# An RWKV and neighbourhood-attention layer: small matmul jobs moved between stages, GpSimd products moved to VectorE, filler matmuls redistributed

## The chip, the cores and the metric

The kernel runs on one core of one Trainium2 chip. The metric is the device time of one execution in microseconds (us). The engines, with the short names of the profile, are TensorE (PE; its weight loads are PEld), VectorE (DVE), ScalarE (ACT), GpSimd (POOL) and SyncE (SP), which here issues nearly all the DMAs.

## The reference

One layer for 128 context tokens and 512 latent tokens, 640 in all, with D = 1024. A normed and modulated input is projected; one part of the projection feeds neighbourhood attention, another an RWKV-7 recurrence of eight heads, run forwards and backwards; both are gated, merged, projected out, and a gated feed-forward network follows.

```python
def _wkv_step(s, inp):
    r, w, k, v, a, b = inp
    sa = jnp.einsum("bhvk,bhk->bhv", s, a)
    s = s * w[:, :, None, :] + sa[..., None] * b[:, :, None, :] + v[..., None] * k[:, :, None, :]
    return s, jnp.einsum("bhvk,bhk->bhv", s, r)
```

The context part starts from a zero state and returns its final states, the latent part starts from given states. In both directions k and the decay differ. All arithmetic is fp32; large products are made of three matmuls on operands split into a high and a low part.

## The kernel before, in words

The 640 tokens are ten chunks of 64. The recurrence is done chunk by chunk: within a chunk it needs the inverse of a unit triangular 64 x 64 matrix, and between chunks a state is carried. A group `ct` of four is two heads (128 partitions). The ten chunks in two directions are 20 "lines". All of this lies in the block `s3`, and for each `ct` has these stages:

- `main`: loads the start states, and the **n jobs** (`n_job`, L990 on) compute the matrices to be inverted, on TensorE, for the lines in three lumps of 8, 8 and 4 (`parts8`). ScalarE copies each result to `Nt` (L1001). They need `AG`, which `akr` (L979) makes on VectorE.
- `inv`: VectorE transposes `Nt` to `RL` (L1082) and eliminates in 30 steps (L1096, L1110 with L1114, L1103); each step is a few VectorE instructions, each of which needs the one before. Then `RT` and `T` (L1123, L1125). At three steps given by `jobs` a lump of further matmuls is placed on TensorE: **v jobs** (transposes of v, copied by ScalarE to `ZV` at L1042; those of backward lines, `flip`, read what the forward lines wrote), **t jobs** (transposes of `BK`, copied to `TG` at L1065), and a **Gram lump** (`g_job`, L1010 and L1013). VectorE multiplies the lump by masks (L1020, L1023) `md` steps after it. After the steps come two small matmul rounds (L1135, L1150) that complete the inverse; I call this stretch the tail.
- `carry`: eight steps over the chunks. In each, TensorE multiplies by `AG` (L1181), ScalarE copies (x0, L1184), TensorE multiplies by the inverse (L1206), ScalarE copies to `ZV` (L1212), TensorE sums the next state (L1219) and the output (L1236), and VectorE scales the state by the decay (L1231), which the next step's L1181 reads.
- Beside the carry runs `prep` for the next group (`prep_a`, `prep_b`): decays by a scan, normed keys, `NK`, `BK`, `bv`. Its pieces are emitted between carry steps, as many as the budgets `bud` allow for ScalarE and VectorE. At the eighth step `last()` emits what is left of it, then `akr` and `r_` of the next group. Two products of each `prep_b` were GpSimd's: the second half of `BK` (L655) and, in the second direction, `bv` (L663).
- `out`: group norm, bonus and gate of the group, emitted beside the next group's `main` and `inv`, as is `bonus` (L962 to L970).

**Fillers.** Independent large matmuls (L173, tiles `fl`) are put between all of this: gates (g), the k, r and v projections of the next group, and the merge with the attention output (a, b). They are units of 48 (g, k, r, v), 24 (a) and 18 (b) matmuls in the fixed order `PRM["order"]`. `stream` hands them out one at a time; `weave` goes through the stage's generator and takes from `plan`, for every `yield`, a group `fillers.out.bonus` (in the carry `fillers.budget`). A unit can have to wait for a mark (v of the next group waited for the end of `inv`), and `need` pulls a unit through where its result is wanted. What follows a unit's matmuls on ScalarE and VectorE (a copy, a shift at L492 to L495, the merge at L1319 and L1322) is emitted some ticks later (`later`, `tick`). The next unit's weights are split on ScalarE (L154) and GpSimd (L155, a "cast") when an eighth of the current unit is done.

The order on every engine is the order in which the instructions are written (`tc.manual_schedule` for this block), so an instruction that waits holds all behind it on its engine. The attention output is loaded back by `o_load` when the last gate is done, just ahead of unit a0. Behind the block come the last merge (`last_gen`) and the projections, where TensorE is near full.

## Time and profile before

| | |
|---|---|
| time, median of 3 runs | 1306.46 us (1304.97 to 1311.55) |
| the profiled execution | 1306.15 us, its span 1304.4 us |
| PE busy | 1224.4 us, 94% |
| DVE busy | 677.3 us, 52% |
| ACT busy | 468.5 us, 36% |
| POOL busy | 282.5 us, 22% |
| mean granted clock of PE | 0.976 |
| block s3 in the span | about 281 to 760 us |

Times of rows are us from the start of the span. In a timeline row stand start, duration, engine, line, operation, output and inputs, shapes and count, and in brackets the idle time of the engine before it and what ended that. In a row of groups stand count, busy us, mean ns of one, and after the second bar the idle time before them.

### The profile page before, as it was taken

What the parts mean: (1) busy time and instruction counts of PE and PEld (TensorE: products, weight loads), DVE (VectorE), ACT (ScalarE), POOL (GpSimd) and SP (SyncE); (2) the same over time, 40 slices, a digit from 0 to 9 for tenths busy, and PEclk for the clock granted to TensorE, in tenths of its full rate; (3) what the DMA queues carried; (4) which work ended last, traced back from release to release, by engine and by line L of the source; (5) the groups of instructions that cost most, each with busy time, mean ns of one, the idle gap of its engine ahead of it and who ended that gap; (6) DMA issues with size and microseconds to landing.
All of it is one profiled execution on the core that took longest, in us unless ns stands there. A gap on an engine that the chain in (4) does not pass through costs nothing.

```text
span 1304.4 us, 27117 instructions
## 1 busy us (share of the span) xinstructions
PE 1224.4 (94%) x11418; PEld 1072.4 (82%) x11418; DVE 677.3 (52%) x1464; ACT 468.5 (36%) x969; POOL 282.5 (22%) x296
## 2 busy tenths in 40 slices
PE   6999999998898797989879989999999999999998
PEld 4688667688887696888768868899999889999987
DVE  4654566647647945874675294643333234333332
ACT  4544455644353345435422341632232111222210
POOL 1231455353223223322321570300000000000000
PEclk8999999999898999989989999999999999999999
DMA  9423975331111121121152472222122222122221
GB/s 347 148 71 123 295 235 166 126 117 45 54 47 49 59 65 44 34 88 45 38 208 89 131 277 82 97 81 82 66 74 88 66 80 81 65 66 95 68 90 41
DMA packets 54130, 134.36 MB, mean 103 GB/s; under 512 B 6868, under 2 KB 21716, under 8 KB 51960
## 3 DMA queue, kind: packets, MB, share of 16 engines
q1 hardware_dynamic: 53144, 131.43, 30.2%
q8 instruction: 90, 1.47, 0.5%
q10 hardware_dynamic: 864, 1.20, 0.3%
q14 instruction: 32, 0.26, 0.1%
HBM read 118.28 MB, written 14.32 MB: 102 GB/s over the span
## 4 chain that ended last, share of the span: by engine, by line
PE 51%; DVE 6%; issue 1%; ACT 1%; DMA 1%; POOL 1%; SPq 0%; DVEq 0%; ACTq 0%; POOLq 0%
PE f L173 24%; PE acc L260 15%; PE fl L173 5%; DVE pr L1110 1%; DVE RL L1114 1%; DVE vp L493 1%; PE w L1181 1%; DMA o<-o_d 1%; PE w L1219 0%; PE w L1193 0%; PE w L1206 0%; PE w L1135 0%; PE w L998 0%; PE w L1013 0%; DVE AG L979 0%
## 5 line engine op out<-in xcount | busy, mean ns | idle before, releaser
L173 PE MATMUL f<-h,whi 128*128 128x256 f32 (+1 forms) x1408 | 306.3, 309 | 0.6 <-POOL h L163 0.6
L173 PEld LDWEIGHTS f<-h,whi 128*128 128x128 f32 x1408 | 236.6, 189 | 1.1 <-POOL h L163 1.0
L154 ACT CAST whi<-wst 128x1024 fp32r<-128x1024 f32 (+2 forms) x134 | 132.3, 990 | 241.9 <-PE acc L260 108.6
L173 PE MATMUL f<-h,wlo 128*128 128x384 f32 (+1 forms) x704 | 217.6, 309 | 0.0
L155 DVE TENSOR_TENSOR wlo<-wst,whi 128x1024 fp32r<-128x1024 f32 x95 | 118.7, 1252 | 178.5 <-ACT whi L154 178.2
L173 PE MATMUL fl<-h,whi 128*128 128x320 f32 x736 | 180.4, 327 | 4.4 <-ACT U L487 3.3
L173 PEld LDWEIGHTS fl<-h,whi 128*128 128x128 f32 x736 | 129.1, 196 | 9.6 <-ACT U L487 3.5
L173 PEld LDWEIGHTS f<-h,wlo 128*128 128x128 f32 x704 | 133.0, 189 | 0.0
L173 PE MATMUL fl<-h,wlo 128*128 128x320 f32 x368 | 120.6, 328 | 1.4 <-POOL wlo L155 1.4
L155 POOL TENSOR_TENSOR wlo<-wst,whi 128x1024 fp32r<-128x1024 f32 (+2 forms) x39 | 79.6, 2041 | 161.8 <-ACT whi L154 158.7
L260 PE MATMUL acc<-whi,ul 128*128 128x512 f32 (+1 forms) x230 | 88.6, 385 | 0.0
L260 PE MATMUL acc<-whi,uh 128*128 128x512 f32 (+1 forms) x230 | 88.3, 386 | 0.0
L260 PE MATMUL acc<-wlo,uh 128*128 128x512 f32 (+1 forms) x230 | 88.2, 386 | 0.0
L260 PE MATMUL acc<-whi,h 128*128 128x512 f32 x240 | 80.6, 409 | 0.7 <-DVE h L369 0.7
L173 PEld LDWEIGHTS fl<-h,wlo 128*128 128x128 f32 x368 | 72.1, 196 | 4.3 <-POOL wlo L155 1.7
L173 PE MATMUL fl<-o,whi 128*128 128x320 f32 x224 | 57.3, 335 | 8.3 <-DMA o<-o_d 5.4
L173 PE MATMUL mm<-h,whi 128*128 128x320 f32 x256 | 63.9, 327 | 0.4 <-ACT pre L576 0.4
L1231 DVE TENSOR_TENSOR ZV<-w,Dt 64x128 f32<-64x128 f32 x64 | 18.4, 288 | 79.8 <-PE w L1219 78.6
L1611 DVE SCALAR_TENSOR_TENSOR a<-a,f 128x384 f32<-128x384 f32 (+1 forms) x44 | 21.5, 488 | 69.6 <-PE f L173 69.5
L260 PEld LDWEIGHTS acc<-whi,h 128*128 128x128 f32 x240 | 45.4, 191 | 14.0 <-issue 2.4
L260 PE MATMUL acc<-whi,m 128*128 128x512 f32 x160 | 53.0, 407 | 0.6 <-POOL m L1498 0.4
L162 ACT CAST uh<-a 128x384 fp32r<-128x384 f32 (+1 forms) x44 | 20.1, 458 | 87.6 <-DVE a L1611 87.6
(315 smaller groups left out, 2290.2 us busy)
## 6 DMA issues: line engine op xcount, KB each, us to landing
wst<-in_w_dram SPq DMA_DIRECT2D x66, 512.0 KB
wa<-in_w_ada_dram SPq DMA_DIRECT2D x16, 1024.0 KB
wst<-in_w_rw_dram SPq DMA_DIRECT2D x31, 512.0 KB
wst<-in_w_qkv_dram SPq DMA_DIRECT2D x12, 512.0 KB
o<-o_d SPq DMA_DIRECT2D x14, 320.0 KB
x<-in_xs_dram SPq DMA_DIRECT2D x8, 512.0 KB
wa<-in_w_ada_dram SPq DMA_DIRECT2D x16, 256.0 KB
wa<-in_w_ada_dram SPq DMA_DIRECT2D x8, 512.0 KB
```

Of the source, the lines that this page charges most:

```text
L154: act.copy(hi[:, :n], st[:, :n])
L155: (eng or dve).tensor_tensor(out=lo[:, :n], in0=st[:, :n], in1=hi[:, :n].bitcast(F32), op=ALU.subtract)
L162: act.copy(hi, src)
L173: pe.matmul(ps[:, :t1 - t0], w[:, a:a + 128], x[:, k0 + kt, t0:t1], start=n == 0, stop=n == 3 * nk - 1)
L260: pe.matmul(pss[i][:, a:b], x[:, kt, ts_], w[:, cs_], start=ki == 0 and n == 0, stop=ki == last and n == 2)
L493: dve.scalar_tensor_tensor(out=o, in0=U[:, u - 1:u - 1 + n], scalar=col("mu0", ci), in1=o, op0=ALU.mult, op1=ALU.add)
L1110: dve.tensor_tensor(out=prv, in0=V(RL[:, s + 1 + a, :], [[32, b - a], [0, s]], s), in1=V(RL[:, s, :], [[0, b - a], [1, s]]), op=ALU.mult)
L1114: dve.tensor_tensor(out=dst, in0=dst, in1=prv, op=ALU.add)
L1181: pe.matmul(px[hrows[h], g * 64:g * 64 + 64], AG[:, l, h, :], ZV[:, l, h, :], start=True, stop=True)
L1231: dve.tensor_tensor(out=V(ZV[own, l + 1, h, :], [[128 * dl, 2], [1, 64]]), in0=V(pn[own, :], [[64, 2], [1, 64]], 64 * g), in1=V(Dt[own, 0, ...
L1611: dve.scalar_tensor_tensor(out=a, in0=a, scalar=0.5, in1=p3[:, :n], op0=ALU.mult, op1=ALU.mult)
```

## The change

- v and t jobs leave the steps of `inv` and stand in `main`, ahead of the n jobs. The v jobs go by the ranges `partsv`, so that the flip of lines 10 and 11 is one of them and no longer part of a t job. v of the next group now waits for the bonus alone (`vR`).
- The Gram lumps are placed after steps 1, 5 and 9 instead of 2, 9 and 16, and their masks three steps later instead of two.
- For ct 1 to 3 the products of L655 and L663 are VectorE's, each with a cost of 0.8 in the budget; so is the addition of the merge at L1322.
- The plan: for ct 0 to 2 `main` has 12 fillers instead of 28, `inv` 231 or 233 instead of 165, `carry` 76 instead of 128 (the six after each step are gone). For ct 3 `main` has 16 instead of 24, `inv` 200 as before, `carry` 124 instead of 128.
- A flag `quiet` stands from the end of a carry to step 4 of the next inversion; while it does, the next unit's cast is asked for only 16 matmuls before the current unit ends.
- `out` has one more `yield` per half for ct 0 to 2, so its GpSimd product is emitted a step later.

```diff
@@ -30,36 +30,36 @@   (PRM: plan of ct 0, then ct 1; ct 2 is as ct 1)
     plan=(
         "24 1 0 0 1 1 1 1 1 1 1 1 0 15",
-        "14.0 0.0 0.0 0.0 14.0",
-        "0.0.0 10.0.0 2.0.1 10.0.0 2.0.0 2.0.1 2.0.1 2.0.1 2.0.1 2.0.1 10.0.0 2.0.0 2.0.0 2.0.0 2.0.0 2.0.0 "
-        "2.0.0 10.0.0 2.0.0 2.0.0 2.0.0 2.0.0 2.0.0 2.0.0 2.0.0 2.0.0 2.0.0 2.0.0 2.0.0 2.0.0 5.0.0 24.0.0 "
-        "20.0.0 10.0.0 8.0.0 0.0.0 8.0.0 0.0.0",
-        "10.0 0.0 8.1 6.2 0.0 8.1 6.2 0.0 8.1 6.2 0.0 8.1 6.2 0.0 8.1 6.2 0.0 8.1 6.2 0.0 8.1 6.2 0.0 8.1 6.2 "
+        "4.0 0.0 0.0 0.0 0.0 0.0 0.0 0.0 0.0 0.0 0.0 8.0",
+        "0.0.0 8.0.0 0.0.1 0.0.0 4.0.0 21.0.1 0.0.1 0.0.1 9.0.1 23.0.1 0.0.0 5.0.0 5.0.0 16.0.0 6.0.0 6.0.0 "
+        "5.0.0 6.0.0 6.0.0 6.0.0 5.0.0 6.0.0 6.0.0 6.0.0 5.0.0 6.0.0 6.0.0 6.0.0 5.0.0 4.0.0 4.0.0 4.0.0 "
+        "16.0.0 10.0.0 8.0.0 0.0.0 8.0.0 0.0.0",
+        "6.0 0.0 8.1 0.2 0.0 8.1 0.2 0.0 8.1 0.2 0.0 8.1 0.2 0.0 8.1 0.2 0.0 8.1 0.2 0.0 8.1 0.2 0.0 8.1 0.2 "
         "6.0",
...
-        "12.2 0.0 0.0 0.0 12.0",
+        "6.2 0.0 0.0 0.0 0.0 0.0 0.0 0.0 0.0 0.0 0.0 10.0",
...
-    jobs=(2, 9, 16), bud=((1.8, 0.8), (1.3, 1.8)), off=6, tk=2, md=2, h3=1, h4=1.07, g1=2)
+    jobs=(1, 5, 9), bud=((1.8, 0.8), (1.3, 1.8)), off=6, tk=2, md=3, h3=1, h4=1.07, g1=2)
@@ -652,16 +652,16 @@
         dve.scalar_tensor_tensor(out=BK[:, :, 0, :], in0=c64(NK[:, 0, :]), scalar=-0.5, in1=c64(Pin),
                                  op0=ALU.mult, op1=ALU.mult)
         yield 0, 1.3
-        pool.tensor_tensor(out=BK[:, :, 1, :], in0=c64(NK[:, 1, :]), in1=c64(Pin), op=ALU.mult)
-        yield 0, 0
+        (dve if ct else pool).tensor_tensor(out=BK[:, :, 1, :], in0=c64(NK[:, 1, :]), in1=c64(Pin), op=ALU.mult)
+        yield 0, 0.8
         if d == 0:
             S.bv = bv_t()
             for (a, b) in parts(ct, "pa"):
                 act.copy(S.bv[:, a:b], NK[:, 1, a:b])
                 yield 0.9 * (b - a) / 640, 0
         else:
-            pool.tensor_tensor(out=S.bv, in0=S.bv, in1=V(NK[:, 1, :], [[-1, 640]], 639), op=ALU.add)
-            yield 0, 0
+            (dve if ct else pool).tensor_tensor(out=S.bv, in0=S.bv, in1=V(NK[:, 1, :], [[-1, 640]], 639), op=ALU.add)
+            yield 0, 0.8
 
 
     with s1:
@@ -983,6 +983,7 @@
                               op=ALU.mult)
 
         parts8 = ((0, 8), (12, 20), (8, 12))
+        partsv = ((0, 8), (8, 10), (12, 20), (10, 12))
 
         def sq(t, n):
             return V(t[:, :], [[64, n], [1, 64]])
@@ -1029,7 +1030,7 @@
 
             if l0 > 9:
                 return flip(l0, l1)
-            n = min(l1, 10) - l0
+            n = l1 - l0
             pv = wps()
             for l in range(l0, l0 + n):
                 for h in range(2):
@@ -1063,13 +1064,15 @@
                                   start=True, stop=True)
             for h in range(2):
                 act.copy(TG[:, l0:l1, h, 0, :], sq(pt[h], n))
-            if l0 == 8:
-                flip(10, 12)
 
         def main(ct, S):
             for h in range(2):
                 sp.dma_start(V(ZV[hrows[h], 0, h, :], [[12 * 128, 2], [1, 64]]), stt[hrows[h], ct, :, :])
                 pool.memset(ZV[hrows[h], 8:11:2, h, :], 0.0)
+            for f, ls in ((v_job, partsv), (t_job, parts8)):
+                for l in ls:
+                    f(S, *l)
+                    yield
             for l in parts8:
                 n_job(S, *l)
                 yield
@@ -1114,9 +1117,8 @@
                         dve.tensor_tensor(out=dst, in0=dst, in1=prv, op=ALU.add)
                 if s - PRM["md"] in jobs:
                     masks()
+                quiet[0] = s < 4
                 if s in jobs:
-                    for f in (v_job, t_job):
-                        f(S, *jobs[s])
                     masks = g_job(S, *jobs[s])
                 yield
             RT = V(f5()[:, :], [[32, 32], [1, 32]])
@@ -1265,6 +1267,8 @@
                 pe.matmul(ps[:, :H2], S.gup, lg_[:, hs_], start=True, stop=True)
                 yield
                 dve.tensor_tensor(out=yc[:, hs_], in0=ps[:, :H2], in1=yc[:, hs_], op=ALU.mult)
+                if ct < 3:
+                    yield
                 if not hf:
                     if ct < 3:
                         yo = kp.tile([P, 643], F32R, tag="pre", bufs=4, name=nm("yo"))[:, :NT], yc
@@ -1319,7 +1323,7 @@
                     dve.scalar_tensor_tensor(out=(mt[c8] if g == "a" else t)[:, a:b], in0=t[:, a:b], scalar=1.0,
                                              in1=ps[:, :b - a], op0=ALU.add, op1=ALU.mult)
                     if g == "b":
-                        pool.tensor_tensor(out=mt[c8][:, a:b], in0=mt[c8][:, a:b], in1=t[:, a:b], op=ALU.add)
+                        dve.tensor_tensor(out=mt[c8][:, a:b], in0=mt[c8][:, a:b], in1=t[:, a:b], op=ALU.add)
 
                 later(rest, (0, 0.5))
 
@@ -1339,7 +1343,7 @@
 
         marks = {None}
         wait = {f"k{c}": f"M{c - 1}" for c in range(1, 4)}
-        wait.update({f"{x}{c}": f"{y}{c - 1}" for c in range(1, 4) for x, y in ("rR", "vI")})
+        wait.update({f"{x}{c}": f"{y}{c - 1}" for c in range(1, 4) for x, y in ("rR", "vR")})
         wait.update({f"a{i}": "A3" for i in range(4, 8)})
         wait.update({f"b{i}": "O2" for i in range(8)})
         done = set()
@@ -1360,9 +1364,10 @@
                     yield False
                 n, f = us[i][0], us[i][3]
                 cast(i)
-                it = f(ws[i])
+                it, asked = f(ws[i]), False
                 for j in range(n):
-                    if j == n // 8:
+                    if not asked and (j >= n // 8 and not quiet[0] or j >= n - 16):
+                        asked = True
                         later(lambda i=i: cast(i + 1), (1.05, 0), -off[0])
                     next(it)
                     tick(1)
@@ -1449,7 +1454,7 @@
 
                 hold[0] = True
                 weave(carry(ct, S, last), (pg,), PRM["bud"])
-                hold[0] = False
+                hold[0], quiet[0] = False, True
                 og = out(ct, S)
                 S = S2
             weave(og)
```

More of the change, by code (lines that the diff above doesn't have):

```diff
@@ L444, in body @@
     o3 = []
-    pend, off, hold = [], [0], [False]
+    pend, off, hold, quiet = [], [0], [False], [False]
     def later(fn, cost=(0.5, 0), more=0):
```

13 lines of the change are left out of this document (removed), and 13 rows, old and new, of the table plan.

## The prediction

> **What bounds the kernel now.** I read the page first (busy time, chain of waits), then the windows of the stages that the change touches, then the timelines of VectorE, GpSimd and ScalarE inside them.
>
> ```profile
> PE 1224.4 (94%) x11418; PEld 1072.4 (82%) x11418; DVE 677.3 (52%) x1464; ACT 468.5 (36%) x969; POOL 282.5 (22%) x296
> PE 51%; DVE 6%; issue 1%; ACT 1%; DMA 1%; POOL 1%; SPq 0%; DVEq 0%; ACTq 0%; POOLq 0%
> ```
>
> TensorE is busy for 94% and leads the chain, so only stretches where it idles or runs at a low clock can be won. They lie in the RWKV part. For each of the four head groups (ct 0 to 3) the windows stand in the order inversion, its tail (from the last transposes to the first carry matmul), carry, transition to the next group. Columns: window, length, busy us of PE, PEld, DVE, ACT, POOL with counts, granted clock, DMA share, GB/s.
>
> ```profile
> 298.60:337.40 38.80, 33.75 (x629) 31.85 (x627) 33.14 (x128) 13.51 (x29) 10.73 (x14) 1.00 0.15 51
> 337.40:352.10 14.70, 12.62 (x198) 12.11 (x198) 9.41 (x16) 3.88 (x9) 0.53 (x1) 0.77 0.17 54
> 352.10:390.50 38.40, 36.86 (x546) 32.49 (x545) 13.98 (x28) 21.73 (x62) 9.85 (x10) 1.00 0.16 50
> 390.50:406.80 16.30, 12.66 (x231) 11.18 (x231) 13.73 (x14) 6.89 (x12) 7.38 (x5) 0.82 0.13 44
> 406.80:454.60 47.80, 39.34 (x655) 36.00 (x654) 40.23 (x135) 16.61 (x37) 12.02 (x16) 0.99 0.14 49
> 454.60:468.70 14.10, 12.77 (x203) 11.97 (x201) 11.42 (x16) 5.01 (x10) 3.83 (x3) 0.76 0.28 89
> 468.70:507.30 38.60, 37.18 (x548) 32.52 (x547) 12.97 (x26) 19.98 (x56) 6.85 (x7) 1.00 0.17 54
> 507.30:526.30 19.00, 12.85 (x239) 11.71 (x239) 14.71 (x15) 9.06 (x17) 8.39 (x6) 0.82 0.12 38
> 526.30:567.00 40.70, 37.63 (x652) 34.93 (x650) 36.38 (x135) 15.57 (x33) 12.90 (x13) 1.00 0.17 58
> 567.00:581.20 14.20, 12.25 (x198) 11.71 (x198) 9.61 (x17) 5.89 (x13) 6.84 (x6) 0.76 0.16 45
> 581.20:617.80 36.60, 36.60 (x548) 32.46 (x547) 14.12 (x27) 20.80 (x59) 8.23 (x9) 1.00 0.21 66
> 617.80:635.50 17.70, 14.43 (x254) 12.81 (x254) 13.77 (x13) 9.76 (x19) 7.07 (x6) 1.00 0.08 26
> 635.50:691.70 56.20, 45.25 (x675) 41.15 (x674) 38.31 (x139) 12.99 (x27) 16.55 (x15) 0.91 0.43 148
> 691.70:704.20 12.50, 11.71 (x204) 11.00 (x202) 9.07 (x17) 3.75 (x8) 2.56 (x2) 1.00 0.28 80
> 704.20:737.20 33.00, 32.94 (x516) 28.52 (x515) 9.87 (x28) 9.22 (x31) 8.58 (x10) 1.00 0.28 83
> ```
>
> The carries belong to TensorE (96 to 100% busy), the inversions to VectorE's chain of 30 steps (84 to 89% busy, 68% in ct 3), the transitions to a serial chain over VectorE. TensorE idles 5.1, 2.1, 1.5, 3.6 us in the first four rows, 50 us in all fifteen.
>
> **Part by part.** One filler matmul is worth 4.01/26 = 0.154 us:
>
> ```profile
> 524.87 4.01 PE fl L173 x26
> ```
>
> *Inversions 0 to 2.* VectorE idles in them for 5.7, 7.6 and 4.3 us (length minus busy). The longest waits are for a Gram lump of which the masks stand only two steps later, behind v jobs, t jobs and ten fillers on TensorE:
>
> ```profile
> 416.34 1.39 DVE L1020 TENSOR_TENSOR AG<-w,K 64x512 f32<-64x512 f32 x2 [3.52 <-PE w L1010]
> ```
>
> With v and t jobs gone from there, no filler ahead of a lump's masks but those of steps already passed, and masks three steps later, lumps are ready in time; the waits of the bonus and of out() stay. I leave 2 us of idle in each: -3.7, -5.6, -2.3, together -11.6. Against it: 66 more fillers in each (165 becomes 231) bring the r chunk's shift inside, four VectorE instructions, two like this one and two of a quarter of its size (0.35, an estimate between 0 and 0.75), 2.2 us, three times, +6.6:
>
> ```profile
> 565.53 0.75 DVE L493 SCALAR_TENSOR_TENSOR kt__613<-U,C,kt__613 128x512 f32<-128x512 f32 x1
> ```
>
> The 198 are four units of 48, so four more GpSimd weight casts (L155) come among the steps. A cast can hold a step up, or can itself be held up:
>
> ```profile
> 430.07 2.46 POOL L155 TENSOR_TENSOR wlo<-wst,whi 128x1024 fp32r<-128x1024 f32 x1 [5.48 <-ACT whi L154]
> 548.91 5.73 POOL L155 TENSOR_TENSOR wlo<-wst,whi 128x1024 fp32r<-128x1024 f32 x1 [7.14 <-ACT whi L154]
> ```
> ```profile
> 430.63 2.22 DVE L1110 TENSOR_TENSOR pr<-RL 128x108 f32<-128x108 f32 x2
> 437.00 0.45 DVE L1110 TENSOR_TENSOR pr<-RL 128x108 f32<-128x108 f32 x2
> ```
>
> The first cost VectorE 1.8 us (2.22 against 0.45), the second next to nothing while taking 5.73 us itself. So four casts cost 0 to 7; I take 5, nearer the upper end since most casts begin in a gap of VectorE. The inversions thus come out at 0 in sum. The Trainium skill ("GPSIMD Engine Reference", Key points) says that GpSimd shares its SBUF interfaces with VectorE and contends with its instructions that have two SBUF inputs, which the steps have. By that rule each cast would cost about its own length, some 10 us in all; the row at 548.91 disagrees, the one at 430.63 agrees. Does TensorE now bound them?
>
> ```profile
> L1062 PE MATMUL w<-K,f 64*64 64x64 f32 x640 | 14.0, 221 | 0.4 <-DVE AG L1020 0.3
> ```
>
> It is busy for 33.8 to 39.3 us there, gains 66 x 0.154 = 10.2 and loses the t jobs (14.0/4 = 3.5) and about as much for the v jobs: 37 to 43, against VectorE's 39 to 47 (the lengths now, as nothing is won in sum, ct 1 shorter and ct 2 longer). Near balance, which is what the slower rival lives on.
>
> *Tails.* Three run at clock 0.76 to 0.77 and last 14.1 to 14.7 us; the fourth at 1.00 lasts 12.5. With filler up to step 30 TensorE doesn't cool before them: -1.8 each, -5.4. Ten fillers ahead of the first carry step become six, four times 0.6: -2.5.
>
> *Carries 0 to 2.* Six fillers between two steps become none. A step:
>
> ```profile
> 612.08 0.40 PE L1236 MATMUL w<-TG,ZV 128*64 128x64 f32 x8
> 612.30 0.61 DVE L1231 TENSOR_TENSOR ZV<-w,Dt 64x128 f32<-64x128 f32 x2 [3.69 <-PE w L1219]
> 613.50 0.45 PE L1181 MATMUL w<-ZV,AG 128*64 128x64 f32 x8
> ```
>
> The next step needs ZV, done at 612.91; it now starts at 613.50. Without the fillers it starts 0.5 us earlier, not 0.9: 7 steps give 3.7 us. What was a cushion is gone: where a prep instruction of the next group stands ahead of L1231 on VectorE or of the x0 copy on ScalarE, the step waits. Bounds: 0 to 3.7; I take 2.2 each, -6.6. BK's and bv's products, now on VectorE, lie inside its 22 to 26 us of idle there.
>
> *Transitions.* GpSimd's two products run against akr:
>
> ```profile
> 394.30 2.08 POOL L655 TENSOR_TENSOR f<-NK,pre 128x640 f32<-128x640 f32 x1 [5.67 <-DVE NK L646]
> ```
> ```profile
> 394.87 8.01 DVE L979 TENSOR_TENSOR AG<-kk,P 64x640 f32<-64x640 f32 x4
> 519.48 3.36 DVE L979 TENSOR_TENSOR AG<-kk,P 64x640 f32<-64x640 f32 x4
> ```
>
> 4.65 us of L979 are contention (in the other two transitions it falls on the v shift). On VectorE the two products take twice the 0.82 of the like L652, 1.6:
>
> ```profile
> L652 DVE SCALAR_TENSOR_TENSOR f<-NK,pre 128x640 f32<-128x640 f32 x8 | 6.5, 818 | 0.0
> L1042 ACT COPY ZV<-w 64x512 f32<-64x512 f32 x16 | 9.3, 581 | 25.0 <-PE w L1036 12.6 <-PE w L1050 12.3
> L1065 ACT COPY TG<-w 128x512 f32<-128x512 f32 x16 | 8.5, 582 | 0.2 <-PE w L1062 0.2
> ```
>
> so -3.0. But v and t jobs now stand ahead of the n jobs, on TensorE and, with their copies, on ScalarE, where the Nt copies wait behind them, and the transposes for those. Now: v shift over at 519.56, transposes at 526.34, 6.8 us.
>
> ```profile
> 518.81 0.75 DVE L495 SCALAR_TENSOR_TENSOR vp<-U,C,vp 128x512 f32<-128x512 f32 x1
> 526.34 1.25 DVE L1082 STREAM_TRANSPOSE RL<-Nt 128x1024 f32<-128x1024 f32 x1 [1.91 <-ACT Nt L1001]
> ```
> ```profile
> 523.18 3.06 ACT L1001 COPY Nt<-w 128x512 f32<-128x512 f32 x3 [8.55 <-PE w L998]
> ```
>
> Then: first v matmuls 0.9, about 6 us of copies (per group four of 0.58 on each of L1042 and L1065 and some smaller ones), about 0.5 while the flip waits, Nt 3.06: 10.5. That is +3.7. Bounds: 0 (hidden behind akr, which takes 3.36 on VectorE at the same time) to 3.7; I take the upper end, since the copies are in one queue. Three times -3.0 + 3.7: +2. In ct 0 the same chain follows the fillers directly; ten fewer fillers save 1.5, and the chain adds 4.5: +3.
>
> *Inversion 3.* 17.9 us idle. Two of its waits:
>
> ```profile
> 645.48 1.39 DVE L1020 TENSOR_TENSOR AG<-w,K 64x512 f32<-64x512 f32 x2 [3.56 <-PE w L1013]
> 658.51 0.69 DVE L1256 TENSOR_TENSOR out<-out,w 128x512 f32<-128x512 f32 x1 [7.43 <-PE w L950]
> ```
> ```profile
> PE fl L173 <- DMA o<-o_d: 5.4, 3, 4.1
> ```
>
> a0's first fillers wait for o's load and hold L950 behind them. Afterwards L950 and the second lump come ahead of a0; only the last lump and out()'s products stay behind. Of the 7.4 and 3.6 some 10 go; 4.5, the length of the wait for the load, less what is done meanwhile, come back at L1256 and L1267. -5.5 (bounds: -11 and 0).
>
> *End.* The plans leave 34 fillers, not 16, for after the last out(): 18 x 0.154 = +2.8. The merge's product moves into VectorE's 23 us of idle in the fourth carry and costs nothing; without that cover it would be 16 times some 0.5.
>
> **Sum:** 0 - 5.4 - 2.5 - 6.6 + 2 + 3 - 5.5 + 2.8 = -12. The profiled execution took 1306.15 (span 1304.4), 0.3 below the median of the runs; that gives 1294.
>
> **Rivals.**
> *The casts cost nothing and half of the copies hide behind akr* (chance 0.22). The row at 548.91 speaks for it; against it, the row at 430. -5 and -6 more, 1283.
> *The gain is given back* (0.19). Copies cost 3.7, the carry's cushion is used up (0 instead of -6.6), and the tails stay cold because TensorE waits for VectorE there anyway (0.9 of 5.4 kept): -1, 1305. The fillers moved are then idle time moved.
> *The inversions become bound by filler* (0.14), the slower side. A filler unit must wait for its weights, cast late while the quiet flag stands (16 fillers, 2.5 us, ahead of need, where GpSimd's part alone took 2.46 and 5.73 above), and for its shift, which is queued among VectorE's steps. It decides from the point where TensorE's 37 to 43 us plus these waits exceed VectorE's 39 to 47. With three unit changes of 4 us each an inversion would take 53: 14, 5 and 12 us over now, +31 - 12 = +19, 1325. Against it: TensorE idles 5.1, 8.5 and 3.1 us in these windows now.
> *The clock falls in the carries* (0.02). Holes of half a microsecond in each step leave TensorE some 87% busy; were the clock halved there, 3 x 30 us of matmuls would add up to 90 us, 1383. The first window is 87% busy in pieces and kept clock 1.00. The Trainium skill ("TensorE: Matmul & The Clock Gate", A second HAM failure mode: psum-queue depth-cycling) reports that such short idle times made the clock swing; that window disagrees.
> My forecast has the remaining 0.43, with its own range 1287 to 1301.
>
> **How the numbers follow.** A change under 0.5% (6.5 us) can't be told from none. Faster (under 1300): 0.22, 0.40 of the forecast's 0.43 and 0.03 of the third case: 0.65. Slower (over 1313): most of the two last: 0.13. Same: 0.22. The range reaches down past 1283 and up past 1305, 1279 to 1311; outside are the slower cases and the far end of the second.
>
> **What would show it.** Right: L979 at 3.4 us for four in all three transitions; no wait of L1020 for L1010 over 1 us; tails at clock 1.00 and about 12.5 us; carry steps of about 3.8 us with L1181 right after L1231; in ct 3 L1256 waiting under 3 us. Wrong: L1082 following the v shift in 7 us (copies hidden), or L1110 at over 1 us beside most casts, or L173 waiting for wlo or for VectorE's shift for several us per inversion (filler-bound), or a clock below 1 in the carries.

## The result, and the profile after

The changed kernel took 1324.73 us (median of 4 runs, 1322.06 to 1327.10), the kernel before beside it 1307.19 us: a ratio of 1.0129, with an interval of 1.0095 to 1.0164. It is slower by 1.3%; the forecast was 1294 us.

The first part of the page of the changed kernel, and its chain of waits by engine:

```profile
PE 1231.3 (93%) x11418; PEld 1078.9 (82%) x11418; DVE 694.1 (53%) x1489; ACT 469.0 (36%) x969; POOL 248.5 (19%) x271
...
PE 49%; DVE 6%; ACT 2%; issue 1%; DMA 1%; POOL 1%; SPq 0%; ACTq 0%; DVEq 0%; POOLq 0%
```

The matmuls are the same 11418. Span less busy time, TensorE stands still for 1320.3 - 1231.3 = 89.0 us (before 1304.4 - 1224.4 = 80.0), and the same matmuls take 6.9 us longer (1231.3 against 1224.4), at a mean clock of 0.970 against 0.976. So the 15.9 us of the span are some 9 us of standing and 7 us of clock. All four runs of the changed kernel have a clock of 0.965 to 0.970; the runs of the kernel before lie at 0.971 to 0.978.

The same stages of the changed kernel as the prediction shows of before (inversion, tail, carry, transition; columns as there). Line numbers of the changed kernel are one to three higher in the rows that follow: L1082 has become L1085, L1110 L1113, L1231 L1233.

```profile
301.10:341.80 40.70, 36.59 (x448) 35.13 (x446) 39.46 (x132) 10.18 (x19) 13.76 (x15) 1.00 0.25 82
341.80:355.10 13.30, 11.32 (x193) 10.78 (x194) 7.49 (x12) 3.89 (x9) 0.14 (x1) 0.74 0.05 15
355.10:394.20 39.10, 33.30 (x504) 28.69 (x503) 17.97 (x32) 22.08 (x61) 8.37 (x9) 0.91 0.14 43
394.20:411.60 17.40, 14.74 (x460) 13.17 (x461) 8.13 (x12) 10.54 (x22) 0.00 (x0) 1.00 0.04 13
411.60:460.90 49.30, 42.86 (x474) 40.15 (x472) 45.45 (x139) 14.21 (x28) 18.73 (x18) 0.94 0.22 76
460.90:474.30 13.40, 11.48 (x192) 10.96 (x192) 7.44 (x12) 3.46 (x8) 1.01 (x2) 0.71 0.16 52
474.30:506.80 32.50, 31.43 (x504) 27.15 (x503) 12.80 (x27) 19.53 (x56) 4.99 (x7) 1.00 0.13 37
506.80:531.40 24.60, 16.44 (x455) 14.70 (x456) 13.01 (x16) 13.28 (x28) 3.02 (x3) 0.86 0.07 23
531.40:579.30 47.90, 42.32 (x479) 39.61 (x477) 43.22 (x138) 13.39 (x28) 14.59 (x17) 0.99 0.22 74
579.30:593.20 13.90, 11.93 (x192) 11.43 (x192) 7.50 (x12) 4.51 (x9) 3.37 (x3) 0.68 0.19 64
593.20:630.60 37.40, 32.94 (x504) 28.21 (x503) 15.31 (x28) 20.53 (x58) 4.95 (x7) 0.95 0.10 30
630.60:652.80 22.20, 17.34 (x475) 15.31 (x476) 12.41 (x16) 13.97 (x30) 2.71 (x3) 1.00 0.05 15
652.80:703.30 50.50, 40.60 (x428) 36.67 (x428) 38.60 (x137) 7.00 (x13) 13.95 (x14) 0.86 0.44 153
703.30:718.50 15.20, 14.01 (x209) 12.90 (x208) 9.34 (x16) 3.75 (x8) 2.56 (x2) 0.89 0.35 111
718.50:751.50 33.00, 32.94 (x517) 28.57 (x516) 11.10 (x30) 9.34 (x31) 5.28 (x5) 1.00 0.23 68
```

Length after less length before, by stage:

| stage | ct 0 | ct 1 | ct 2 | ct 3 | sum | predicted |
|---|---|---|---|---|---|---|
| inversion | +1.9 | +1.5 | +7.2 | -5.7 | +4.9 | 0 for ct 0 to 2, -5.5 for ct 3 |
| tail | -1.4 | -0.7 | -0.3 | +2.7 | +0.3 | -5.4 - 2.5 |
| carry | +0.7 | -6.1 | +0.8 | 0 | -4.6 | -6.6 |
| transition | +1.1 | +5.6 | +4.5 | | +11.2 | +2 |

With 2.5 ahead of the first inversion (predicted +3) and 1.6 behind the last carry (568.8 against 567.2; predicted +2.8) that makes the 15.9 of the span. The places of the loss are the transitions (9 more than predicted), inversions 0 to 2 (10.6 more) and the tails (8 more).

**A transition.** VectorE between the v shift and the transposes of the third inversion, in the timeline of the changed kernel:

```profile
516.26 0.75 DVE L495 SCALAR_TENSOR_TENSOR vp<-U,C,vp 128x512 f32<-128x512 f32 x1
516.92 3.37 DVE L979 TENSOR_TENSOR AG<-kk,P 64x640 f32<-64x640 f32 x4
...
531.44 1.25 DVE L1085 STREAM_TRANSPOSE RL<-Nt 128x1024 f32<-128x1024 f32 x1 [9.55 <-ACT Nt L1002]
```

and ScalarE at the same time:

```profile
519.16 1.76 ACT L1043 COPY ZV<-w 64x512 f32<-64x512 f32 x4 [6.50 <-PE w L1037]
...
522.40 1.73 ACT L1043 COPY ZV<-w 64x512 f32<-64x512 f32 x4 [1.48 <-PE w L1051]
524.06 2.61 ACT L1066 COPY TG<-w 128x512 f32<-128x512 f32 x6
527.25 2.29 ACT L1002 COPY Nt<-w 128x512 f32<-128x512 f32 x2 [0.59 <-PE w L999]
530.72 0.69 ACT L1002 COPY Nt<-w 128x256 f32<-128x256 f32 x1 [1.17 <-PE w L999]
```

The v shift is over at 517.0, the transposes start 14.4 us later; before it was 6.8, predicted 10.5. The first copy of the v jobs starts 2.15 us after the shift, the v and t jobs' copies are 6.1 us and those of Nt 3.0, and in between ScalarE waits for TensorE three more times (1.48, 0.59 and 1.17 us; the copies of the t jobs don't wait). VectorE does its L979 in 3.37 us and then stands for 9.55.

**A cast.** VectorE in the third inversion, and GpSimd at the same time:

```profile
553.17 2.66 DVE L1113 TENSOR_TENSOR pr<-RL 128x117 f32<-128x117 f32 x2
...
556.13 0.46 DVE L1113 TENSOR_TENSOR pr<-RL 128x112 f32<-128x112 f32 x2
```
```profile
553.17 2.51 POOL L155 TENSOR_TENSOR wlo<-wst,whi 128x1024 fp32r<-128x1024 f32 x1 [6.52 <-ACT whi L154]
```

A pair that takes 0.46 (of 112 columns, here 117) takes 2.66 when a cast starts with it: VectorE is kept from its work for 2.2 of the cast's 2.51 us. I added up how much longer each VectorE instruction of inversions 0 to 2 is than the shortest of its kind, where GpSimd works beside it: 14 us before, 26 after, +12 (predicted +5). In both, 2.8 us of it lie beside the four splits of L163; the casts have 11.4 us before, 9 of them, and 23.6 after, 14 of them.

**The end of an inversion.** Windows of 3.41 us around the end of the first inversion of the changed kernel:

```profile
335.52:338.93 3.41, 2.17 (x15) 1.90 (x13) 3.41 (x9) 0.00 (x0) 2.55 (x3) 1.00 0.17 59
338.93:342.34 3.41, 0.00 (x0) 0.00 (x0) 3.34 (x20) 0.00 (x0) 0.00 (x0) 1.00 0.47 154
342.34:345.75 3.41, 1.97 (x64) 1.98 (x66) 3.36 (x4) 0.46 (x2) 0.00 (x0) 0.50 0.00 0
345.75:349.17 3.42, 3.42 (x34) 3.35 (x31) 2.62 (x7) 1.65 (x4) 0.00 (x0) 0.50 0.16 53
```

TensorE has used up its filler while VectorE still works through the last steps and the first transposes. A whole window without a matmul is followed by two at half clock.

**A carry.** VectorE, GpSimd and TensorE in the first carry of the changed kernel:

```profile
385.19 2.88 DVE L495 SCALAR_TENSOR_TENSOR vp<-U,C,vp 128x512 f32<-128x512 f32 x1
388.11 0.61 DVE L1233 TENSOR_TENSOR ZV<-w,Dt 64x128 f32<-64x128 f32 x2
```
```profile
385.19 2.34 POOL L155 TENSOR_TENSOR wlo<-wst,whi 128x1024 fp32r<-128x1024 f32 x1 [21.76 <-ACT whi L154]
```
```profile
388.45 1.01 PE L1183 MATMUL w<-ZV,AG 128*64 128x64 f32 x8 [4.44 <-DVE ZV L1233]
```

Here a cast holds a prep instruction of 0.75 us for 2.88; L1233 stands behind it, and TensorE, without filler between the steps, stands for 4.44 us, 2.1 of them for the cast and most of the rest for the v shift itself. This carry has clock 0.91.

### The profile page after: what moved, and what is told of

Same layout as the page of the kernel before. It is cut to its first block, busy times and chain, and to the rows that moved or that the text cites. A ratio compares the mean times of both kernels' runs of the same rounds, so it can differ in the third digit from the quotient of the medians.

```text
span 1320.3 us, 27118 instructions
## 1 busy us (share of the span) xinstructions
PE 1231.3 (93%) x11418; PEld 1078.9 (82%) x11418; DVE 694.1 (53%) x1489; ACT 469.0 (36%) x969; POOL 248.5 (19%) x271
## 4 chain that ended last, share of the span: by engine, by line
PE 49%; DVE 6%; ACT 2%; issue 1%; DMA 1%; POOL 1%; SPq 0%; ACTq 0%; DVEq 0%; POOLq 0%
PE f L173 24%; PE acc L260 15%; PE fl L173 5%; DVE pr L1113 1%; DVE RL L1117 1%; PE w L1208 0%; PE w L1183 0%; PE w L1221 0%; PE fl L1498 0%; PE w L1137 0%; DMA o<-o_d 0%; PE w L1152 0%; DVE f L1125 0%; PE w L1195 0%; PE w L1201 0%
## 5 line engine op out<-in xcount | busy, mean ns | idle before, releaser
L155 POOL TENSOR_TENSOR wlo<-wst,whi 128x1024 fp32r<-128x1024 f32 (+2 forms) x39 | 76.6, 1964 | 217.6 <-ACT whi L154 196.5
L173 PE MATMUL fl<-o,whi 128*128 128x320 f32 x224 | 57.5, 338 | 12.7 <-DVE mt L1323 5.5
L1233 DVE TENSOR_TENSOR ZV<-w,Dt 64x128 f32<-64x128 f32 x64 | 18.5, 289 | 70.8 <-PE w L1221 69.7
L173 PEld LDWEIGHTS fl<-o,whi 128*128 128x128 f32 x224 | 39.4, 199 | 17.1 <-issue 5.8
L1113 DVE TENSOR_TENSOR pr<-RL 128x52 f32<-128x52 f32 (+5 forms) x192 | 53.3, 318 | 0.1
```

The source lines that it names most:

```text
L155: (eng or dve).tensor_tensor(out=lo[:, :n], in0=st[:, :n], in1=hi[:, :n].bitcast(F32), op=ALU.subtract)
L173: pe.matmul(ps[:, :t1 - t0], w[:, a:a + 128], x[:, k0 + kt, t0:t1], start=n == 0, stop=n == 3 * nk - 1)
L1113: dve.tensor_tensor(out=prv, in0=V(RL[:, s + 1 + a, :], [[32, b - a], [0, s]], s), in1=V(RL[:, s, :], [[0, b - a], [1, s]]), op=ALU.mult)
L1233: dve.tensor_tensor(out=V(ZV[own, l + 1, h, :], [[128 * dl, 2], [1, 64]]), in0=V(pn[own, :], [[64, 2], [1, 64]], 64 * g), in1=V(Dt[own, 0, ...
```

## The experiments

Theory A was: the loss is the order of the v and t jobs in the transitions, and the casts on GpSimd. Theory B: the filler's new places make the inversions filler-bound. Times are medians of 4 to 12 runs; all ratios are to the kernel before, measured beside each group (1306.9 to 1308.4 us).

| kernel | us | ratio | interval |
|---|---|---|---|
| e1_n_first | 1326.94 | 1.0154 | 1.0106 to 1.0201 |
| e2_old_fill | 1323.47 | 1.0125 | 1.0088 to 1.0162 |
| e3_products | 1304.09 | 0.9977 | 0.9957 to 0.9998 |
| e4_dve_casts | 1309.35 | 1.0019 | 0.9998 to 1.0039 |
| e5_best_try | 1306.09 | 0.9988 | 0.9978 to 0.9999 |
| e6_vt_lumps | 1323.94 | 1.0130 | 1.0108 to 1.0152 |
| e7_fill_only | 1318.95 | 1.0090 | 1.0071 to 1.0109 |
| e8_no_quiet | 1325.71 | 1.0132 | 1.0109 to 1.0154 |
| e9_early_lumps | 1319.92 | 1.0091 | 1.0069 to 1.0114 |
| e10_late_lumps | 1316.75 | 1.0071 | 1.0051 to 1.0091 |
| e11_late_old_fill | 1314.70 | 1.0056 | 1.0036 to 1.0075 |
| e12_fill_gap | 1310.16 | 1.0024 | 1.0010 to 1.0037 |
| e13_keep_busy | 1300.12 | 0.9938 | 0.9920 to 0.9955 |
| e14_vt_only | 1313.73 | 1.0044 | 1.0028 to 1.0061 |
| e15_after_busy | 1319.36 | 1.0088 | 1.0061 to 1.0116 |
| e16_keep_busy2 | 1294.97 | 0.9893 | 0.9873 to 0.9913 |
| e17_busy_dve_casts | 1296.14 | 0.9905 | 0.9886 to 0.9925 |

### The order in the main stage

```
         def main(ct, S):
...
+            for l in parts8: n_job(S, *l); yield
             for f, ls in ((v_job, partsv), (t_job, parts8)): ...
-            for l in parts8: n_job(S, *l); yield
```

> The changed kernel with one thing moved: in the main stage the n jobs are issued ahead of the v and t jobs. Theory A (the cost of the transitions is the ScalarE copies of the v and t jobs standing ahead of the copies into Nt, for which the transposes wait): the chain from the v shift to the transposes goes back from 14.5 us to 6.8 to 8 us, three transitions and the first main stage gain some 2.5 to 5 us each, 1308 to 1316 us. Theory B (the filler's new places in the inversions are the cause, the transitions only show work that is pushed about): what is saved in the transitions comes back as inversions that are as much longer, 1322 to 1327 us.

1326.94 us, no gain: this half of theory A falls, and as theory B said, what the transitions save comes back in the inversions. The transitions do become 6 to 8 us shorter (9.6, 17.3 and 16.3 us), but inversions 0 to 2 get 7 us longer each, the fourth 6. VectorE in the timeline of this kernel:

```profile
298.39 1.25 DVE L1085 STREAM_TRANSPOSE RL<-Nt 128x1024 f32<-128x1024 f32 x1 [3.88 <-issue]
...
308.56 1.39 DVE L1021 TENSOR_TENSOR AG<-w,K 64x512 f32<-64x512 f32 x2 [6.27 <-PE w L1011]
```

The wait for the Nt copies has become a wait at the first masks: the first Gram lump stands behind the same jobs on TensorE and ScalarE. Later lumps, with the casts on VectorE too, were to hide it:

```
-    jobs=(1, 5, 9), bud=((1.8, 0.8), (1.3, 1.8)), off=6, tk=2, md=3, ...
+    jobs=(6, 11, 16), bud=((1.8, 0.8), (1.3, 1.8)), off=6, tk=2, md=4, ...
```

with the order of e1 and the casts of e4 (below), and in e11 the old filler too.

> The changed kernel with the n jobs ahead of the v and t jobs, casts of the g, k, r and v units on VectorE, and the lumps at steps 6, 11 and 16 with masks four steps later, so that VectorE has some ten steps to do before it needs the first masks. Theory G (with the n jobs first, the same 6.2 us of ScalarE copies became a wait of 6.2 to 6.7 us at the first masks): these waits go, PE idles 10 us less than with the casts alone (1309.4 us), 1298 to 1304 us. If filler then sets the inversions' length: 1308 to 1314 us.

> As the late-lump kernel, with the filler's counts per stage and places of the kernel before. If full inversions (231 units) are what is left of the loss: 1295 to 1300 us. If TensorE then stands idle in the inversions for want of filler: 1305 to 1315 us.

1316.75 us, above both ranges, and 1314.70 us: 7 and 5 us worse than the casts alone (e4). VectorE in the third inversion of the late-lump kernel:

```profile
532.82 1.22 DVE L155 TENSOR_TENSOR wlo<-wst,whi 128x1024 fp32r<-128x1024 f32 x1 [7.72 <-ACT whi L154]
```

The wait has moved once more: VectorE now stands in front of a cast whose first half is queued on ScalarE behind the same copies. In all three places that I tried for this block, something in order behind it waits some 6 to 8 us. The filler's count (e11) changes little.

### The casts, and holding them back

For the g, k, r and v units:

```
-                return 48, lambda: wdma(w_rw[15 + i]), lambda w: wcast(w, pool), \
+                return 48, lambda: wdma(w_rw[15 + i]), lambda w: wcast(w, dve), \
```

> The changed kernel with the weight casts of the g, k, r and v units on VectorE instead of GpSimd. Theory A (each cast on GpSimd beside the inversion's VectorE work costs VectorE some 2.2 us, more than doing it itself): 1311 us. The rival (a cast costs VectorE its own 0.5 to 1.2 us and what GpSimd did was nearly free): 15 us longer, 1340 us.

1309.35 us, 15.4 less than the changed kernel. The windows of inversions 0 to 2:

```profile
305.50:343.40 37.90, 34.97 (x392) 33.45 (x385) 36.75 (x137) 9.38 (x18) 1.03 (x10) 1.00 0.22 74
411.10:456.40 45.30, 42.18 (x473) 40.00 (x473) 40.69 (x142) 14.21 (x28) 4.82 (x13) 0.97 0.20 69
525.30:570.10 44.80, 41.73 (x479) 39.55 (x477) 40.76 (x143) 13.49 (x27) 4.87 (x13) 1.00 0.22 75
```

VectorE has 9.9 us less to do in them (118.2 against 128.1 us) though it makes the casts itself, and they are 9.9 us shorter. This half of theory A stands.

```
-                quiet[0] = s < 4
...
-                hold[0], quiet[0] = False, True
+                hold[0] = False
```

> The changed kernel without the holding back of casts: a cast is asked for at an eighth of the unit before it, as in the kernel before. If holding back is what lays the casts on VectorE's dense steps: 1310 to 1318 us. If the casts cost the same wherever they fall in an inversion: 1322 to 1328 us.

1325.71 us: holding the casts back over the first steps makes no difference.

### The three operations, and the casts in the kernel before

In the kernel before, the product, and in the same way bv's addition and the merge; e5 adds the casts of e4:

```
-        pool.tensor_tensor(out=BK[:, :, 1, :], in0=c64(NK[:, 1, :]), in1=c64(Pin), op=ALU.mult)
+        (dve if ct else pool).tensor_tensor(out=BK[:, :, 1, :], in0=c64(NK[:, 1, :]), in1=c64(Pin), op=ALU.mult)
```

> The kernel before with only the three operations moved from GpSimd to VectorE (the product into BK, the r shift, the merge addition; the first two not in the first chunk). Theory A (the shifts of the v columns then run without GpSimd beside them, 3 us a transition): 1298 us. Theory C (VectorE is the engine that the inversions wait for, and pays 1.1 to 2.2 us for each): 1312 us.

> The kernel before with the three operations of the products run on VectorE (1304.1 us by themselves) and the weight casts of the g, k, r and v units on VectorE too. If the casts on GpSimd stall VectorE in the kernel before as they do in the changed one (contention 14.8 us in its inversions 0 to 2 against 27.1 us, where taking them away gave 15.4 us): 8 us less, 1296 us. If the casts stall VectorE only where the changed kernel puts them (held back until the fourth step is past): 1302 to 1306 us.

The operations by themselves gain 3.4 us, less than the 9 expected, but a gain; theory C falls. The casts on top gain nothing (1306.09). So what moving the casts brings depends on the kernel. One reason shows in the profile: on VectorE a cast brings a new wait, as in the second inversion of e5 VectorE stands for 8.3 us in two places (4.9 in the longer) in front of a cast whose first half ScalarE hasn't done; in that inversion of e4 it has no such wait. That a cast on GpSimd can lie in waits that VectorE's chain has anyway in the kernel before would fit as well, but no run separates the two.

### The filler's places

The plan's lines of main stage, inversion and carry, in the changed kernel (e2), and the other way round in the kernel before (e7):

```
-        "4.0 0.0 ... 8.0", "0.0.0 8.0.0 0.0.1 0.0.0 4.0.0 ...", "6.0 0.0 8.1 0.2 ..."
+        "14.0 0.0 ... 14.0", "0.0.0 10.0.0 2.0.1 10.0.0 2.0.0 ...", "10.0 0.0 8.1 6.2 ..."
```

> The changed kernel with the filler's counts per stage and their places as in the kernel before (28 units in a main stage, 165 in an inversion, 128 in a carry, two per step), all other edits kept. Theory B (the filler's places in the inversions make them filler-bound): inversions 0 to 2 go back to or under their lengths of before, 1305 us or less. Theory A (the casts on GpSimd and the order of the v and t jobs are the cause): fewer casts fall into inversions 0 to 2 and VectorE is kept from less, some 8 to 16 us gained of which the transitions give none, 1308 to 1317 us. If neither the count nor the places matter: 1325 us.

> The kernel before with the changed kernel's filler counts and places alone (12 units in a main stage, 231 to 233 in an inversion, 76 in a carry). Theory F (thin carries lose TensorE's clock and time, and fuller inversions are longer by their filler): 1313 to 1322 us. If a unit costs the same wherever it stands: 1304 to 1310 us.

With the old counts and places the changed kernel takes 1323.47 us, the same: as the cause of the loss, theory B falls. What it said of the inversions did come: 0 to 2 last 123.0 us together in this run's profile (137.9 in the changed kernel, 127.3 before), with 8 casts in them instead of 14. But the other stages are as much longer than in the changed kernel: the carries by 4.7 us, the transitions by 4.2, the fourth inversion by 3.5, the tails by 2.4. So the filler decides in which stage the loss stands; with the old places it is the transitions, 68.3 us against 53.0 before. Alone in the kernel before, the new places cost 11.7 us, in theory F's range, though the carries lose nothing. One inversion and one carry of that kernel (e7), windows:

```profile
404.70:462.40 57.70, 49.22 (x714) 45.75 (x712) 42.18 (x138) 19.91 (x42) 17.41 (x18) 0.97 0.19 65
...
476.20:508.70 32.50, 31.42 (x504) 27.16 (x503) 12.07 (x27) 19.27 (x56) 7.28 (x8) 1.00 0.12 38
```

The inversion is 9.9 us longer than before (47.8), the carry 6.1 shorter: with the v and t jobs still in the inversion, 66 fillers more give TensorE 49.2 us of work there, more than the whole inversion lasted. With them gone it has room, and the places are neutral in sum.

### The v and t jobs, and the lumps

All in the kernel before. The first two parts of this edit are e14, all of it is e6, the last alone e9; e6 also lets the v units start at the carry's end, as the changed kernel does:

```
         def main(ct, S):
...
+            for f, ls in ((v_job, partsv), (t_job, parts8)):
+                for l in ls: f(S, *l); yield
...
-                    for f in (v_job, t_job):
-                        f(S, *jobs[s])
...
-    jobs=(2, 9, 16), ... md=2
+    jobs=(1, 5, 9), ... md=3
```

> The kernel before with the v and t jobs in the main stage, the three Gram lumps at steps 1, 5 and 9 with masks three steps later, and v units waiting for the carry's end only; filler counts and places, products and casts as before. Theory E (this move is what loses: the v and t jobs' ScalarE copies lengthen the transitions by 4 us each, and the inversions don't give it back because VectorE sets their length): 1318 to 1327 us. If the inversions give it back: 1303 to 1308 us.

> The kernel before with the three Gram lumps at steps 1, 5 and 9 and their masks three steps later; the v and t jobs stay in the lumps, all else as before. Theory G (of the two halves of the move, the v and t jobs in the main stage cost the 17 us, 6 us of ScalarE copies put on each transition): 1303 to 1311 us here. If the earlier lumps cost it: 1315 to 1325 us.

> The kernel before with the v and t jobs in the main stage and the Gram lumps left at steps 2, 9 and 16 with masks two steps later. If the v and t jobs' 6 us of ScalarE copies ahead of the n jobs' cost what they cost in the changed kernel: 1318 to 1326 us. If the earlier lumps are the costly half: 1306 to 1311 us.

v and t jobs in the main stage alone (e14): 1313.73 us, +6.2, between its two answers. With the early lumps and the earlier v units (e6): 1323.94, another 10.2. The early lumps alone (e9): +13.0, theory G's second answer. So both halves cost. What the early lumps do is seen at out(), of which the matmuls (L936) then stand behind a lump on TensorE: VectorE's wait for them at L940 is 4.9 and 4.8 us in the second and third inversion of e9, 0.8 in each before, 2.0 in each of e6 and none in e14. Second and third inversion and the transitions behind the second and third carry of e14, windows:

```profile
413.20:453.20 40.00, 34.55 (x409) 31.96 (x408) 39.12 (x135) 10.97 (x23) 11.96 (x16) 0.91 0.16 58
533.00:569.90 36.90, 32.65 (x412) 29.80 (x410) 36.12 (x134) 9.73 (x19) 13.68 (x13) 1.00 0.18 63
...
505.90:533.00 27.10, 20.44 (x479) 18.80 (x479) 14.78 (x16) 15.11 (x31) 8.40 (x6) 0.81 0.08 28
620.50:644.40 23.90, 19.20 (x490) 17.21 (x490) 13.78 (x13) 15.59 (x33) 7.11 (x6) 1.00 0.06 21
```

This shows the exchange by itself: the inversions are 7.8 and 3.8 us shorter, VectorE idle for 0.9 and 0.8 us in them; the transitions are 8.1 and 6.2 us longer, with 6 us more ScalarE work in each (15.11 against 9.06, 15.59 against 9.76). ScalarE stood idle for 25 to 31 us of an inversion; in the transition its copies are on the chain. (The profiled execution of e14 has a span of 1307.9 us, under its median.)

### TensorE's standing, and its clock

e3 with filler moved, for ct 0 and 2; the first pair is the inversion's entry behind the last step, the second one of eight in the carry:

```
-24.0.0
+40.0.0
...
-6.2
+4.2
```

> The kernel before with the three operations on VectorE (1304.1 us), and 16 filler units of carry 0 and of carry 2 moved to the place after the last solve step of the inversion before them, where TensorE stands for 5.2 and 3.9 us. Theory H (a stretch of 3.4 us in which TensorE is under half busy is followed by 3.4 to 6.8 us at half clock, and what fills it is free): carries 3.4 us shorter each, inversions unchanged, one half-clock stretch less each, 1294 to 1298 us. If a unit costs the same wherever it stands: 1304 us.

1310.16 us, 6 us worse than without and outside both ranges. The two carries that gave up 16 fillers each are not shorter (39.0 and 36.5 us; in e3 38.5 and 36.6). VectorE at the end of the first inversion of this kernel (L481, L483 and L1111 here are L493, L495 and L1123 of the kernel before):

```profile
337.15 0.74 DVE L481 SCALAR_TENSOR_TENSOR rt__612<-U,C,rt__612 128x512 f32<-128x512 f32 x1
337.93 0.75 DVE L483 SCALAR_TENSOR_TENSOR rt__612<-U,C,rt__612 128x512 f32<-128x512 f32 x1
338.60 1.90 DVE L1111 STREAM_TRANSPOSE f<-RL 128x1024 f32<-128x1024 f32 x1
```

The 16 fillers finish a projection, and its shift (four instructions, 2.2 us) now stands ahead of the transposes on VectorE: the gap moves with the filler. Filler isn't free where VectorE ends the stage. Matmuls that bring nothing with them are:

```
+        def warm(ps, n):
+            for _ in range(n):
+                pe.matmul(ps[:, 0:256], ident, K[:, 0:256], start=True, stop=True)
...
                 ph = wps()
+                if g == 0:
+                    warm(ph, (11, 0, 8, 0)[ct])
```

and the like ahead of the n jobs (e15: of the v jobs), with the numbers that the expectations give.

> The kernel before with the three operations on VectorE (1304.1 us), and matmuls that compute nothing needed (overwritten by the next ones) where TensorE stands still: 11 and 8 of them after the last solve step of chunks 0 and 2 (5.2 and 3.9 us of standing), 10 ahead of the n jobs of chunk 2 (4.7 us). Theory K (the half clock behind such a stretch is a cost by itself): three stretches of 6.8 us at half clock go, up to 3.4 us each, 1294 to 1300 us. If TensorE's clock in the tails hides behind VectorE and ScalarE work, or the matmuls push what follows: 1303 to 1308 us.

> The changed kernel with the same kind of matmuls: 13, 7 and 12 of them after the last solve step of chunks 0, 1 and 2 (6.1, 3.6 and 5.6 us of standing), 11 ahead of the v jobs of chunk 2 (5.3 us). Theory K: the half-clock stretches of 6.8, 13.7, 6.8 and 10.2 us shrink to a third, 1312 to 1317 us, so that most of what the change lost by the clock comes back. If the clock only follows: 1322 to 1327 us.

> The kernel with idle-time matmuls (1300.1 us) with more of them: 3 and 2 after the last solve step of chunks 1 and 3, 6 and 3 ahead of the n jobs of chunks 1 and 3. If the half clock behind these shorter gaps (1.3 to 3 us) is paid too: 1294 to 1298 us. If the gaps are too short for it and the matmuls push what follows: 1300 to 1304 us.

> The kernel before with the three operations and the casts of the g, k, r and v units on VectorE (1306.1 us), and idle-time matmuls in its own gaps (6, 3, 11 and 2 after the last solve steps; 4, 6 and 3 ahead of the n jobs of chunks 1 to 3). If what the casts gave there was lost again to the clock: 1293 to 1299 us, under the same without the casts moved. If the casts are free in the kernel before: 1299 to 1303 us.

Theory K stands, at the upper edge of its first range. In the kernel before with the three operations such matmuls gain 4.0 us (1300.12), with 43 of them instead of 29 it is 9.1 us (1294.97, 1.1% under the kernel before and the lowest median of all). In the changed kernel 43 of them gain 5.4 us (1319.36), between the two answers. As the kernel before with the three operations gains 9.1 us by as many, these 5.4 us don't count as a part of what the change lost. The four tails of the last but one (e16), windows:

```profile
342.00:356.20 14.20, 13.73 (x206) 12.56 (x204) 9.51 (x16) 3.89 (x9) 0.49 (x1) 0.88 0.12 45
454.00:466.70 12.70, 12.63 (x209) 11.60 (x207) 11.47 (x16) 5.03 (x10) 3.85 (x3) 1.00 0.28 94
562.80:575.40 12.60, 12.09 (x203) 11.07 (x202) 9.73 (x17) 5.91 (x13) 5.98 (x5) 1.00 0.12 43
685.10:697.60 12.50, 12.50 (x210) 11.59 (x208) 9.11 (x17) 3.75 (x8) 2.56 (x2) 1.00 0.25 78
```

Three of them have clock 1.00 and 12.5 to 12.7 us. With the casts on VectorE too (e17, 35 such matmuls) it is 1296.14, inside the first range, but not under e16 as its theory asked: moving the casts again brings nothing in the kernel before, and there is no sign that the clock hid a gain.

## Why the prediction was wrong, step by step

Three steps failed: the casts' +5 in inversions 0 to 2 (12 measured), the +3.7 of the copies' chain in each transition (7.6 and 6.6 in the second and third), and the tails, before which TensorE was not to cool and did.

**Inversions 0 to 2: predicted 0, measured +10.6.** VectorE's idle time fell by 7.8 us (17.6 to 9.8), predicted 11.6. The lumps' masks wait no more, as predicted, but out()'s wait at L940, which was to stay at 0.8, became 1.7 and 2.2 us in the second and third inversion. One wait was read wrongly: in ct 0, 5.3 of the 5.7 us were none for a lump but for ScalarE's share of the k shift, in VectorE's timeline before:

```profile
307.43 0.35 DVE L493 SCALAR_TENSOR_TENSOR kt__613<-U,C,kt__613 128x128 f32<-128x128 f32 x1 [5.33 <-ACT kt__613 L492]
```

e14 still has it; in the changed kernel it is 0.7 us, so that this term came out right by luck. The r shift's term (+6.6) holds: of VectorE's 18.4 us more (128.1 against 109.8) some 6 are left beside contention. The term that failed is the casts' +5, "nearer the upper end since most casts begin in a gap of VectorE": it is +12, with 14 casts in the three inversions instead of 9, at 1.7 us each instead of 1.3. That they cost the time, too, e4 shows (15.4 us in all stages). The Trainium skill ("GPSIMD Engine Reference", Key points) has the rule of contention with instructions of two SBUF inputs that I set against the row at 548.91 and then left out; the row at 553.17 agrees with it (2.66 us instead of 0.46).

**Transitions: predicted +2, measured +11.2.** The relief came: in the first transition L979 takes 3.37 us instead of 8.01,

```profile
397.49 3.37 DVE L979 TENSOR_TENSOR AG<-kk,P 64x640 f32<-64x640 f32 x4
```

and in the second the v shift ahead of it 4.3 us instead of 6.7. The chain's +3.7 was mis-sized: from v shift to transposes 14.4 us, not 10.5, which is +7.6. I had counted the copies (6.1 and 3.0 us, as predicted), but 0.9 us for the first v matmuls, which took 2.15, and 0.5 for the wait ahead of the flip, where flip and n jobs make ScalarE wait three times, 3.2 us in all. Another order didn't help (e1, e10). In the kernel before this block of work was cut into three lumps.

**Tails: predicted -7.9, measured +0.3.** "With filler up to step 30 TensorE doesn't cool before them" was wrong about the change, not about the clock. The filler still ends before VectorE does; TensorE stands for 6.09 us there in ct 0 (5.24 before) and goes to half clock. The fourth tail, at 1.00 before, fell to 0.89 and got 2.7 us longer. Where TensorE is really kept busy and the clock stays at 1.00 (three tails of e16), the tail is 12.5 to 12.7 us, which is the -1.8 per tail that the step had. What the four fillers fewer gave can't be told apart.

**Carries: predicted -6.6, measured -4.6.** Ct 1 gave 6.1, beyond the upper bound of 3.7; ct 0 and ct 2 gave nothing, for the reason the step named ("what was a cushion is gone"). In ct 0 what strikes is the v shift with a cast beside it, above; in ct 2 it is prep on ScalarE ahead of the x0 copy (L1186). TensorE's waits for that copy in this carry, us in all, times, longest:

```profile
PE w L1208 <- ACT x L1186: 3.5, 3, 1.6
```

The rival that priced a fall of the clock in the carries at 1383 had the sign right for ct 0 and 2 (0.91 and 0.95) and the size wrong by far: single windows fall, not the stage.

**Right:** inversion 3 (-5.7 for -5.5), with its mechanism: L1256 (now L1258) waits 2.7 us instead of 7.4, L1020 for L1013 no more instead of 3.6, and 2.1 come back at L1267 (now L1269). The end (+1.6 for +2.8). In number also ct 0's main stage (+2.5 for +3), but that may be luck: in the profiles of e15 and e8, which are the same program up to there, the first inversion starts at 303.0 and 305.0 us instead of 301.1.

**The rivals.** The filler-bound one had the time, 1325, but not the mechanism: it made VectorE wait 31 us more in inversions 0 to 2, where its waits fell by 7.8, and with the filler back in its old places (e2) the time is the same. "The gain is given back" was nearest in kind, and too mild. None had contention above the bound of 7: it is five casts more at 1.7 us each (23.6 us over 14 casts), and the nine old ones at 1.7 instead of 1.3 (11.4 over 9). Of the signs of being wrong that were named, L1110 (now L1113) at over 1 us beside a cast and a clock below 1 in carries came; transposes 7 us behind the v shift did not.

What the parts come to, alone or one on the other: v and t jobs +6.2, early lumps with the earlier v units on top +10.2, the three operations -3.4, the filler's places and the holding back of casts about nothing on top of these: +13 of the 17.5. The remaining 4 were not pinned to an edit; the further `yield` in out() was tried in no run. The 15.4 us of the casts are no part of this sum, since no edit of the change moved them to another engine.

## What to carry to other kernels

Ahead of moving work out of a stage, ask which engine's queue in the new place has no room: here 6 us of ScalarE copies left a stage with 25 us of room for a chain that had none. What a neighbour's contending operation costs must be tried in the kernel at hand: moving the same casts to VectorE gained 15.4 us in the changed kernel and nothing in the kernel before. Filler moved to another stage can move a loss without changing its size. Where TensorE must stand for 1.3 to 5.2 us, a handful of matmuls that nobody needs can pay: 43 of them, 0.45 us each (11 in 4.91 us), gained 9 us.

## What the runs showed of the hardware

I had not expected how sharp the clock is. I cut the traces of six kernels (before, after, e4, e13, e14, e16) into the 3.41 us grid on which the clock changes, and took TensorE's busy share of each piece from its matmul records. Of 45 pieces under 40% busy, all were followed by half clock; between 40 and 60%, 25 of 52; above 60%, 34 of some 2090, and most of these 34 ran at half clock themselves. The Trainium skill ("TensorE: Matmul & The Clock Gate", Part 1: The HAM clock gate, What's actually happening) gives a window of 3413 ns and two states, full and half. The trace agrees with both (0.50 and 1.00, steps of 3.41 us). The page says that an idle window brings the half rate; here one that is a third busy does it as well.
